# Expert weights into the [i1, i2, token] table: word writes by index in place of one-hot products

## The chip, the core and the metric

The kernel runs on one core of a Trainium2 chip. The metric is the device time of one execution in microseconds (us). The engines are named as in the profile: PE (TensorE, the matrix engine; PEld its weight loads), DVE (VectorE), ACT (ScalarE), POOL (GpSimd, which also issues all DMAs whose addresses come from an index), SP (SyncE, which issues most of the other DMAs). Each engine works through its own program in a fixed order; semaphores hold an instruction back until what it needs is there.

## The reference

One decoder block on 512 tokens of 1024 features, float32. Two mixers (a gated recurrence and dilated window attention) give a new x; behind a second norm (h2) comes the expert layer, which is where the change lies:

```python
q = (x @ w_q).reshape(B, S, 8, 2, 64)
s = einsum('bshpc,hpnc->bshpn', q, sub_keys)          # two halves, 128 keys each
s1, i1 = top_k(s[..., 0, :], 16); s2, i2 = top_k(s[..., 1, :], 16)
# top 16 of the 256 sums; expert number idx = i1 * 128 + i2; gate = softmax
hid = einsum('thkd,td->thk', u[idx], h2)              # 128 experts a token
a   = gelu(hid) * gate
out = einsum('thk,thkd->td', a, v[idx])               # added to x
```

So each token picks 128 pairs (8 heads of 16) out of 16384 experts, takes rows of u and v for them, and two heads of one token may pick the same expert.

## The kernel before, in words

The 512 tokens are four tiles (0 to 3) of 128. The mixers run in two halves (`Front(0)`, `Front(1)`, two tiles each); their weights arrive as 74 loads `w` on SP per half. The merge at the end of a half adds its two branches on POOL (L456, four adds), and what follows (output projection, h2, expert queries) waits for these adds.

The expert layer reaches the rows in two ways. By index: tile 0 gathers its rows of u, tile 3 its rows of u and v. Such a gather (`row`, L618) is one POOL instruction that fetches one row of 4 KB for each of 128 tokens; DVE multiplies and sums it (L626, L645). Streamed: tiles 1 and 2 need u whole, tiles 1, 2 and 0 need v whole. For a block b of 128 experts (128 blocks), `hidden(b)` loads `ub`, splits it into a high and a low half (`uh` on ACT, `ul` by a subtraction), and PE makes 24 products `ph` of 256 columns; ACT's gelu leaves them in `pre`, of which RING places exist. Then the loop over b loads `vb`, splits it into `vh` and `vl`, multiplies `pre[b]` by the gates `Gc` of that block (L825), splits the product into `ah` and `al`, and PE makes 18 products `acc` of 512 columns (L834). The acc products of a block need the gates of all three tiles.

That is what the table `g_d` is for: per token, the gate (tile 0: gate times gelu) of expert [i1, i2], and zero elsewhere. `scatter_steps` makes it from one-hot products: for four tokens at a time DVE compares a row of 0..127 with i1 and i2 (`e12`, L666) and multiplies by the weight's three bfloat16 thirds (`eg`, L670; ACT makes some thirds, L674), PE multiplies one-hot i1 by weighted one-hot i2 (12 products, L680), ACT copies the result to `Gx`, and SP writes `Gx` to DRAM. There are 32 such groups a tile, 96 in all: tile 1's beside the second half's mixers, those of tiles 0 and 2 beside the first `hidden` blocks. Products of one expert picked twice add up in PE.

`routing(T)` finds a tile's experts: DVE's top-16 instructions, `eq` (DVE), `sel` (POOL, L582 and L584) and `idf` (DVE). `Pump` objects (`rows`, `scat`) put steps of gathering and scattering between the other work. The order on each engine is then fixed when the kernel is built, by a scheduler that estimates durations.

Of the kernel before, what the change touches and what calls it, by code (L numbers as in the profile page):

```python
# [11 lines left out]
I32 = mybir.dt.int32  # L12
# [25 lines left out]
# Token tiles by how the expert layer reaches them: rows of u gathered, u streamed whole, v streamed whole.  # L38
# VD starts with UD; the tile that is not in it gathers its rows of v.
# [5 lines left out]
GT = 16  # L45
NGT = NV // GT
GB = 8
# the first weights' low halves are Pool's
LPOOL = 4
# steps of gathering and scattering before the end of the second half's mixers  # L50
ROWS_P, SCAT_PP = 99, 5
# [3 lines left out]
GS, EGB = 4, 2  # L55
ACT3 = {1: (0, 4, 8, 12), 0: (0, 4, 8, 12), 2: (0, 8)}
ROWS_F, ROWS_D, SCAT_F = 3, 2.0, 0.4
UK, WBUFS, ATB = 4, 4, 3

# columns of the packed per-partition parameters  # L60
C_G1, C_HGN, C_LB, C_QG, C_KG, C_END = 0, 8, 9, 17, 18, 19
# columns of the packed shape constants
M_ATT, M_HG, M_END = 0, 512, 640
# slots of the packed dense weights
# [4 lines left out]
def kernel(ctx: ExitStack, tc: tile.TileContext, x, wst, par, cst, cols, g2, keys, u, v, ut, vr, out):  # L69
# [9 lines left out]
    nc.scalar.activation(root, eps[:, 0:1], AF.Sqrt)  # L79
    h2g = {}  # L80
# [17 lines left out]
    def accumulate(out, ws, xs, cut, w_stays):  # L98
        """Sum over the blocks of w x, in three products where they come in two parts."""
# [24 lines left out]
    # lower bound: softmax over the two logit rows, row 0  # L124
# [5 lines left out]
    # values of the first group by token; of the other two with every fourth token's in a row  # L130
# [13 lines left out]
    class Front:  # L144
        """The mixers of one half of the tokens, and the queries of their expert layer."""

        def __init__(self, h, hi_pool, after_unit):
# [5 lines left out]
            for t in range(NT):  # L153
# [5 lines left out]
                for c in range(0, KC, 4):  # L159
# [20 lines left out]
        def slot(self, i, ks=slice(0, KC)):  # L180
            """Row blocks ks of a slot's weights, UK of them in a tile: the blocks' operands in order."""
# [14 lines left out]
        def proj(self, i, x, T):  # L196
            """A slot's 256 columns of the half's products with x, on the partitions (T) or along them."""
# [334 lines left out]
    def routing(T, rq):  # L532
# [66 lines left out]
        if T in VD:  # L599
# [6 lines left out]
            for j in range(2):  # L606
                nc.tensor.transpose(pt[:, 1 + j], i12[:, j], ident)
# [295 lines left out]
```

## Time and profile before

| | us |
|---|---|
| median of 3 timed runs | 1846.65 (1845.62 to 1847.0) |
| span of the profiled execution | 1845.0 |
| PE busy, share of the span | 1674.0, 91% |
| DVE busy | 1444.1, 78% |
| ACT busy | 795.6, 43% |
| POOL busy | 793.6, 43% |

The span runs from the first to the last instruction of the profiled execution; the profile gives no other time of its own for it. Busy time is an average over stages that differ: the first half's mixers fill PE from 0 to about 310 us, the second half's lie from there to about 700 us, the first `hidden` blocks and the scatter to 1066 us, the streamed products with v from 1066 us to the end.

### The profile page before, as it was taken

What the parts mean: (1) busy time and instruction counts of PE and PEld (TensorE: products, weight loads), DVE (VectorE), ACT (ScalarE), POOL (GpSimd) and SP (SyncE); (2) the same over time, 40 slices, a digit from 0 to 9 for tenths busy, and PEclk for the clock granted to TensorE, in tenths of its full rate; (3) what the DMA queues carried; (4) which work ended last, traced back from release to release, by engine and by line L of the source; (5) the groups of instructions that cost most, each with busy time, mean ns of one, the idle gap of its engine ahead of it and who ended that gap; (6) DMA issues with size and microseconds to landing.
All of it is one profiled execution on the core that took longest, in us unless ns stands there. A gap on an engine that the chain in (4) does not pass through costs nothing.

```text
span 1845.0 us, 28370 instructions
## 1 busy us (share of the span) xinstructions
PE 1674.0 (91%) x10573; PEld 1482.8 (80%) x10573; DVE 1444.1 (78%) x2681; ACT 795.6 (43%) x1348; POOL 793.6 (43%) x546
## 2 busy tenths in 40 slices
PE   6999889889789989888867899999999999999987
PEld 6998888667667878777867878888888888888766
DVE  5644547887887758999999977877877788888777
ACT  5655551211114556368756534343343434343232
POOL 3211312463664335556566543344323464444442
PEclk9999999988899989889978899999999999999999
DMA  6453553778787887534455799999988999999887
GB/s 196 153 158 119 175 194 118 270 235 276 244 279 264 297 298 261 183 111 145 152 183 202 238 372 334 339 328 326 367 298 299 345 339 341 340 340 317 288 309 278
DMA packets 169963, 475.61 MB, mean 258 GB/s; under 512 B 14304, under 2 KB 62688, under 8 KB 168800
## 3 DMA queue, kind: packets, MB, share of 16 engines
q1 hardware_dynamic: 112416, 270.56, 43.0%
q0 software_dynamic: 55296, 201.35, 30.9%
q10 hardware_dynamic: 2112, 1.88, 0.3%
q8 instruction: 83, 1.36, 0.3%
q14 instruction: 56, 0.46, 0.1%
HBM read 443.85 MB, written 28.84 MB: 256 GB/s over the span
## 4 chain that ended last, share of the span: by engine, by line
PE 47%; DVE 25%; DMA 11%; issue 9%; POOL 5%; ACT 1%; DVEq 0%; POOLq 0%; SPq 0%; ACTq 0%
PE acc L834 19%; PE pp L109 13%; PE ph L109 10%; DMA row<-in_u_dram,idx 6%; DVE row L626 4%; DVE e L666 4%; DVE eg L670 3%; POOL row L618 3%; DMA Gc<-g_d 3%; PE pg L680 2%; PE pr L680 1%; DVE cs L564 1%; DVE rest L515 1%; DVE ti L514 1%; DVE h2g L645 1%
## 5 line engine op out<-in xcount | busy, mean ns | idle before, releaser
L618 POOL DMA_INDIRECT row<-in_u_dram,idx x206 | 254.9, 1237 | 383.8 <-DVE row L626 274.3
L626 DVE SCALAR_TENSOR_TENSOR row<-row,h2g 128x1024 f32<-128x1024 f32 x206 | 272.4, 1328 | 62.2 <-DMA row<-in_u_dram,idx 61.3
L109 PE MATMUL ph<-hH,uh 128*128 128x256 f32 x1024 | 302.1, 295 | 7.1 <-ACT pre L792 6.0
L109 PE MATMUL ph<-hH,ul 128*128 128x256 f32 x1024 | 302.9, 296 | 5.0 <-POOL ul L95 5.0
L109 PE MATMUL ph<-hL,uh 128*128 128x256 f32 x1024 | 299.0, 292 | 0.0
L834 PE MATMUL acc<-vl,ah 128*128 128x512 f32 x768 | 241.8, 396 | 9.3 <-DVE vl L95 9.3
L834 PE MATMUL acc<-vh,al 128*128 128x512 f32 x768 | 240.0, 393 | 0.0
L94 ACT ACTIVATE uh<-ub 128x1024 fp32r<-128x1024 f32 x128 | 136.7, 1068 | 230.7 <-PE ph L109 214.1
L834 PE MATMUL acc<-vh,ah 128*128 128x512 f32 x768 | 222.5, 395 | 9.9 <-ACT vh L94 9.9
L109 PEld LDWEIGHTS ph<-hH,uh 128*128 128x128 f32 x1024 | 205.9, 201 | 12.8 <-ACT pre L792 7.8
L109 PEld LDWEIGHTS ph<-hH,ul 128*128 128x128 f32 x1024 | 205.5, 201 | 6.3 <-POOL ul L95 5.8
L109 PEld LDWEIGHTS ph<-hL,uh 128*128 128x128 f32 x1024 | 204.6, 200 | 3.8
L680 PEld LDWEIGHTS <-e 128*128 128x128 bf16 x1152 | 124.8, 119 | 73.4 <-DVE eg L670 65.4
L834 PEld LDWEIGHTS acc<-vl,ah 128*128 128x128 f32 x768 | 143.2, 190 | 40.0 <-DVE vl L95 11.8
L834 PEld LDWEIGHTS acc<-vh,ah 128*128 128x128 f32 x768 | 142.9, 190 | 38.2 <-ACT vh L94 10.5
L834 PEld LDWEIGHTS acc<-vh,al 128*128 128x128 f32 x768 | 145.5, 190 | 31.8
L94 ACT ACTIVATE ah<-Gc 128x384 fp32r<-128x384 f32 x128 | 66.9, 523 | 229.4 <-PE acc L834 226.7
L95 DVE TENSOR_TENSOR vl<-vb,vh 128x1024 fp32r<-128x1024 f32 x128 | 156.1, 1219 | 12.2 <-ACT vh L94 12.0
L618 POOL DMA_INDIRECT row<-in_v_dram,idx x76 | 111.6, 1469 | 120.0 <-DVE h2g L645 109.2
L680 PE MATMUL pg<-eg,e 128*128 128x128 bf16 x768 | 103.1, 297 | 51.8 <-DVE eg L670 51.3
L94 ACT ACTIVATE vh<-vb 128x1024 fp32r<-128x1024 f32 x128 | 135.6, 1059 | 28.6 <-DMA vb<-in_vr_dram 27.9
L674 ACT ACTIVATE eg<-e,pk 128x128 bf16<-128x128 bf16 x320 | 115.4, 565 | 70.9 <-DVE e L666 68.1
(279 smaller groups left out, 3582.4 us busy)
## 6 DMA issues: line engine op xcount, KB each, us to landing
w<-in_wst_dram SPq DMA_DIRECT2D x140, 512.0 KB
ub<-in_ut_dram SPq DMA_DIRECT2D x128, 512.0 KB
vb<-in_vr_dram SPq DMA_DIRECT2D x128, 512.0 KB
Gc<-g_d SPq DMA_DIRECT2D x15, 1536.0 KB
g_d<-Gx SPq DMA_DIRECT2D x16, 960.0 KB
g_d<-Gx SPq DMA_DIRECT2D x8, 1024.0 KB
row<-in_u_dram,idx POOLq DMA_INDIRECT x206
sc<-in_x_dram SPq DMA_DIRECT2D x4, 512.0 KB
```

Source lines behind the costliest of these rows:

```text
L94: nc.scalar.activation(hi, x, AF.Copy)
L95: (eng or nc.vector).tensor_tensor(out=lo, in0=x, in1=hi.bitcast(F32), op=ALU.subtract)
L109: nc.tensor.matmul(out, l, r, start=(i == 0), stop=(i == len(ops) - 1))
L514: nc.vector.max_index(out=ids[:, 0:8], in_max=vals[:, 0:8], in_values=src)
L515: nc.vector.match_replace(out=rest[:, :w], in_to_replace=vals[:, 0:8], in_values=src, imm_value=-BIG)
L618: nc.gpsimd.indirect_dma_start(out=r, out_offset=None, in_=src, in_offset=bass.IndirectOffsetOnAxis(ap=index, axis=0))
L626: nc.vector.scalar_tensor_tensor(r, r, 1.0, h2g[T], op0=ALU.mult, op1=ALU.mult, accum_out=hid[:, g, j:j + 1])
L666: nc.vector.tensor_tensor(out=e12, in0=iota[:, None].to_broadcast([P, 2, NKEY, GS]), in1=e[:, 0:2].to_broadcast([P, 2, NKEY, GS]), op=ALU. ...
L670: last_e2[0] = nc.vector.tensor_tensor(out=eg[:, :n], in0=e12[:, 1:2].to_broadcast([P, n, NKEY, GS]), in1=e[:, 2:2 + n].to_broadcast([P, n ...
L674: nc.scalar.activation(eg[:, 2, :, q], e12[:, 1, :, q], AF.Copy, scale=pk3[:, VD.index(T), i + k + q:i + k + q + 1])
L680: nc.tensor.matmul(pt[:, q], e12[:, 0, :, q0 + q], eg[:, j, :, q0 + q], start=(j == 0), stop=(j == 2))
L834: nc.tensor.matmul(acc[t][c], lt, r[:, c * 512:(c + 1) * 512], start=(b == 0 and i == 0), stop=(b == NKEY - 1 and i == 2))
```

## The change

Instead of one-hot products, each pair's weight is written to its place in the table by an indirect DMA of single words. The table is now three tensors [i1, i2, token] of 8 MB, one a tile. They are cleared first: twelve DMAs of 2 MB each from a tile of zeros, issued from ACT's queue behind every fourth weight load of the first half. For pair j of a tile, one DVE instruction compares all 128 expert numbers of a token with that of pair j and sums the weights of the equal ones (`same`, `wsum`), so that all writers of one place write the same sum; then one POOL instruction writes 128 words, one a token, to `place` = expert * 128 + token. That is 128 such pairs of instructions a tile, 384 in all. The 16 writes of a head wait for all 16 of the head before (`behind`), and the loads of `Gc` wait for a tile's last head. `ul` is DVE's in all blocks (before, POOL made it in the first 46), the blocks ahead of the products with v go from 46 to 60 and the places for `pre` from 58 to 72, and some gathers of tile 3 move ahead of the products with v.

```diff
-NPRE, RING = 46, 58
+ROWS_P, SCAT_PP = 99, 110
+NPRE, RING = 60, 72
+ROWS_F, ROWS_H, ROWS_D, SCAT_F = 3, 0.5, 1.9, 3
+RT3 = 16
...
         if T in VD:
-            pt = route_bank(T)
-            i12 = rt.tile([P, 2, P], F32, name="i12")
...
-                thirds(VD.index(T), pt[:, 3])
+            nc.vector.tensor_scalar(place[:, VD.index(T)], full, float(P), tok, op0=ALU.mult, op1=ALU.add)
...
-    def scatter_steps(T, bank):
...
+    def behind(d, others):
+        for o in others:
+            tc.add_manual_dep(d.ins, o.ins.name, mybir.DependencyInfo(mybir.DependencyClass.Sync, mybir.DependencyReason.DATA),
+                              reason="pairs of one expert")
+    def spread_steps(T):
+        i = VD.index(T)
+        w = gates[:, T] if T in UD else hid[:, UG.index(T)]
+        for j in range(P):
+            same = rt.tile([P, P], F32, name="same", bufs=2)
+            nc.vector.scalar_tensor_tensor(same, fulls[:, i], fulls[:, i, j:j + 1], w, op0=ALU.is_equal, op1=ALU.mult,
+                                           accum_out=wsum[:, i, j:j + 1])
+            d = nc.gpsimd.indirect_dma_start(out=g_d[i].rearrange("i j t -> (i j t)")[:, None], in_=wsum[:, i, j:j + 1],
+                                             out_offset=bass.IndirectOffsetOnAxis(ap=place[:, i, j:j + 1], axis=0),
+                                             in_offset=None)
...
+            if j % TOPK == 0:
+                before, spread[i] = spread[i], []
+            behind(d, before)
+            spread[i].append(d)
+            yield 1
...
+        def clearing(load):
+            if f_units[0] % 4 == 3 and clear:
+                g, k = clear.pop(0)
+                with tc.issue_after(load.ins):
+                    nc.scalar.dma_start(out=g[:, k:k + 32].rearrange("p (a b) t -> p a (b t)", b=8),
+                                        in_=zero[:, None].to_broadcast([P, 4, D]))
...
-    scat.add(scatter_steps(1, pr_bank))
+    scat.add(spread_steps(1))
...
+    scat.add(spread_steps(0))
...
-        ubs = halves(us.tile([P, KC, P], F32R, name="uh"), us.tile([P, KC, P], F32R, name="ul"), ub,
-                     nc.gpsimd if b < NPRE else nc.vector)
+        ubs = halves(us.tile([P, KC, P], F32R, name="uh"), us.tile([P, KC, P], F32R, name="ul"), ub)
...
+        scat.add(spread_steps(2))
+        scat(2 * P)
         for b in range(NPRE):
+            if b == RT3:
+                routing(3, rq3)
...
+            for t, g in enumerate(g_d):
+                behind(nc.sync.dma_start(out=Gc[:, t], in_=g[:, b:b + GB]), spread[t])
```

The scheduler lays the engines' programs out anew. On POOL, at the end of the second half's mixers, before (`row` is tile 0's gather, `pairA` the merge's add):

```order
L584 TENSOR_TENSOR sel<-sel 128x400
L618 DMA row<-in_u_dram,idx 128x1024 x18
L456 TENSOR_TENSOR pairA<-pairA,pairB 128x512 x2
L618 DMA row<-in_u_dram,idx 128x1024
L456 TENSOR_TENSOR pairA<-pairA,pairB 128x512
L618 DMA row<-in_u_dram,idx 128x1024
L456 TENSOR_TENSOR pairA<-pairA,pairB 128x512
L618 DMA row<-in_u_dram,idx 128x1024 x12
L95 TENSOR_TENSOR ul<-ub,uh 128x1024 x2
```

Now, at the same place (L599 is the gather, L646 the write of 128 words to tile 1's table, L457 the merge's add):

```order
L599 DMA row<-in_u_dram,idx 128x1024
L646 DMA g_d_113<-wsum,place 2097152x1 x2
L599 DMA row<-in_u_dram,idx 128x1024
L646 DMA g_d_113<-wsum,place 2097152x1 x5
L599 DMA row<-in_u_dram,idx 128x1024 x3
L646 DMA g_d_113<-wsum,place 2097152x1 x16
L599 DMA row<-in_u_dram,idx 128x1024 x3
L646 DMA g_d_113<-wsum,place 2097152x1 x16
L599 DMA row<-in_u_dram,idx 128x1024 x3
L457 TENSOR_TENSOR pairA<-pairA,pairB 128x512 x4
L646 DMA g_d_113<-wsum,place 2097152x1 x11
L599 DMA row<-in_u_dram,idx 128x1024
```

The merge's adds come behind 83 gathers and 48 word writes (39 of these writes stand above), where before 94 gathers and no write stood ahead of the first of them; 80 word writes of tile 1 are still to come. Further down on POOL, beside the first `hidden` blocks, before (`ul` is the low half of a block of u, `Gc` the copy of the table's first blocks):

```order
L687 COPY Gc<-Gx 128x128
L95 TENSOR_TENSOR ul<-ub,uh 128x1024 x2
L582 TENSOR_TENSOR sel<-eq,ci 128x800
L584 TENSOR_TENSOR sel<-sel 128x400
L95 TENSOR_TENSOR ul<-ub,uh 128x1024
L582 TENSOR_TENSOR sel<-eq,ci 128x800
L687 COPY Gc<-Gx 128x128
L95 TENSOR_TENSOR ul<-ub,uh 128x1024
L584 TENSOR_TENSOR sel<-sel 128x400
L582 TENSOR_TENSOR sel<-eq,ci 128x800
L95 TENSOR_TENSOR ul<-ub,uh 128x1024
```

Now (`g_d_115` is tile 0's table, `g_d_114` tile 2's; `row` and `rq` are tile 3's gathers, L574 and L576 its routing):

```order
L646 DMA g_d_115<-wsum,place 2097152x1 x16
L574 TENSOR_TENSOR sel<-eq,ci 128x800
L599 DMA row<-in_u_dram,idx 128x1024 x3
L599 DMA rq<-in_u_dram,idx 128x1024 x2
L576 TENSOR_TENSOR sel<-sel 128x400
L646 DMA g_d_115<-wsum,place 2097152x1 x16
L574 TENSOR_TENSOR sel<-eq,ci 128x800
L599 DMA row<-in_u_dram,idx 128x1024 x3
L599 DMA rq<-in_u_dram,idx 128x1024 x2
L646 DMA g_d_114<-wsum,place 2097152x1
L646 DMA g_d_115<-wsum,place 2097152x1 x16
L646 DMA g_d_114<-wsum,place 2097152x1 x13
```

The `ul` and `Gc` rows are gone from POOL; 384 word writes, the last 57 gathers of tile 0 and the first 45 of tile 3 stand between the first and the last word write of the program. Each Pool DMA also waits on one of eight semaphores, that of the DMA eight before it. On SP, around the first loads of `Gc`:

```order
L770 DMA ub<-in_ut_dram 128x1024 x5
L187 DMA w<-in_wst_dram 128x1024 x4
L770 DMA ub<-in_ut_dram 128x1024 x12
L799 DMA Gc<-g_d_113 128x1024
L770 DMA ub<-in_ut_dram 128x1024 x20
L784 DMA h2g<-h_d 128x1024
L770 DMA ub<-in_ut_dram 128x1024 x41
L799 DMA Gc<-g_d_115 128x1024
L799 DMA Gc<-g_d_114 128x1024
L804 DMA vb<-in_vr_dram 128x1024 x3
L799 DMA Gc<-g_d_113 128x1024
```

The gates of tiles 0 and 2 stand behind 78 loads of `ub`. On PE the same shows as 1776 `ph` products (74 blocks) ahead of the first `acc` product, against 1248 (52 blocks) before.

## Rows read from the trace of the kernel before

**Rows 1.** Busy time by engine in stretches; then PEclk, DMA share, GB/s.

```profile
100.00:200.00 100.00, 100.00 (x1007) 93.71 (x1007) 44.87 (x85) 56.28 (x101) 14.86 (x7) 1.00 0.46 143
760.00:1050.00 290.00, 232.31 (x1737) 220.12 (x1737) 280.10 (x624) 187.66 (x348) 172.13 (x103) 0.87 0.48 161
1060.00:1440.00 380.00, 375.12 (x2135) 328.90 (x2134) 298.62 (x446) 147.97 (x208) 144.32 (x108) 0.99 0.94 333
```

**Rows 2.** PE's waits, 740 to 1066 us: total, times, longest.

```profile
PE pg L680 <- DVE eg L670: 51.3, 25, 9.8
```

**Rows 3.** PE groups from 0 to 1066 us: busy, mean ns, idle before.

```profile
L109 PE MATMUL ph<-hL,uh 128*128 128x256 f32 x416 | 127.2, 306 | 0.0
```

**Rows 4.** PE groups from 1066 us to the end.

```profile
L109 PE MATMUL ph<-hL,uh 128*128 128x256 f32 x608 | 171.9, 283 | 0.0
```

**Rows 5.** Line 834, the products with v: ns min/median/max, first and last start.

```profile
L834 PE MATMUL acc<-vh,ah x768: 387/389/797, 1066.2 to 1832.4; 128*128 128x512 f32 x192
...
L834 PE MATMUL acc<-vh,al x768: 387/389/628, 1074.9 to 1835.1; 128*128 128x512 f32 x192
```

**Rows 6.** Line 666, the first one-hot operand: same columns.

```profile
L666 DVE TENSOR_TENSOR e<-iota,pk x96: 660/686/3107, 567.5 to 1044.1; 128x1024 bf16<-128x1024 bf16 x96
```

**Rows 7.** PE in order of time, 1100 to 1115 us: start, duration.

```profile
1106.02 1.55 PE L834 MATMUL acc<-vh,ah 128*128 128x512 f32 x6
1107.41 0.28 PE L109 MATMUL ph<-hH,ul 128*128 128x256 f32 x1
1107.53 0.28 PE L109 MATMUL ph<-hH,uh 128*128 128x256 f32 x1
```

**Rows 8.** POOL groups over the span.

```profile
L618 POOL DMA_INDIRECT row<-in_u_dram,idx x206 | 254.9, 1237 | 383.8 <-DVE row L626 274.3 <-DVE ti L517 16.8 <-DVE tv L516 16.8
...
L582 POOL TENSOR_TENSOR sel<-eq,ci 128x800 f32<-128x800 bf16 x32 | 54.5, 1704 | 56.1 <-DVE eq L580 55.9
L584 POOL TENSOR_TENSOR sel<-sel 128x400 f32<-128x400 f32 x32 | 40.8, 1276 | 0.7
```

**Rows 9.** POOL in order of time, 655 to 725 us: start, duration, idle before.

```profile
674.66 1.80 POOL L618 DMA_INDIRECT row<-in_u_dram,idx  x1 [4.81 <-DVE row L626]
676.77 0.94 POOL L618 DMA_INDIRECT row<-in_u_dram,idx  x1 [0.30 <-issue]
678.01 0.94 POOL L618 DMA_INDIRECT row<-in_u_dram,idx  x1 [0.30 <-PE pp L109]
```

**Rows 10.** POOL in order of time, 1180 to 1240 us.

```profile
1186.58 1.68 POOL L618 DMA_INDIRECT row<-in_u_dram,idx  x1 [2.71 <-DVE row L626]
1188.56 1.67 POOL L618 DMA_INDIRECT row<-in_u_dram,idx  x1 [0.30 <-issue]
```

**Rows 11.** DVE in order of time, 655 to 760 us.

```profile
682.04 2.69 DVE L626 SCALAR_TENSOR_TENSOR row<-row,h2g 128x1024 f32<-128x1024 f32 x1 [5.15 <-DMA row<-in_u_dram,idx]
```

**Rows 12.** DVE, tile row, 655 to 725 us: ns min/median/max, first and last start.

```profile
L626 DVE SCALAR_TENSOR_TENSOR row<-row,h2g x19: 1210/1225/3326, 663.7 to 720.2; 128x1024 f32<-128x1024 f32 x19
```

**Rows 13.** DMA queues: packets, MB, share of 16 engines' span.

```profile
q1 hardware_dynamic: 112416, 270.56, 43.0%
q0 software_dynamic: 55296, 201.35, 30.9%
```

**Rows 14.** DVE groups, 740 to 1062 us.

```profile
L666 DVE TENSOR_TENSOR e<-iota,pk 128x1024 bf16<-128x1024 bf16 x62 | 75.7, 1227 | 6.8 <-PE pg L680 6.6
L670 DVE TENSOR_TENSOR eg<-e,pk 128x1024 bf16<-128x1024 bf16 x64 | 74.7, 1171 | 0.0
...
L95 DVE TENSOR_TENSOR ul<-ub,uh 128x1024 fp32r<-128x1024 f32 x7 | 9.4, 1346 | 0.0
...
L626 DVE DVE_READ_ACCUMULATOR rq<-rq,h2g 128x1 f32 x17 | 1.3, 76 | 0.0
```

**Rows 15.** Line 605, a 128x128 scalar_tensor_tensor on DVE.

```profile
L605 DVE SCALAR_TENSOR_TENSOR i<-i,full x3: 272/285/293, 399.2 to 883.5; 128x128 f32<-128x128 f32 x3
```

**Rows 16.** Line 456, the merge's adds on POOL.

```profile
L456 POOL TENSOR_TENSOR pairA<-pairA,pairB x8: 1283/1956/2245, 218.3 to 610.8; 128x512 f32<-128x512 f32 x8
```

More of the change, by code (lines that the diff above doesn't have):

```diff
@@ L79 @@
     nc.scalar.activation(root, eps[:, 0:1], AF.Sqrt)
+    tok = const.tile([P, 1], F32, name="tok")
+    nc.scalar.dma_start(out=tok, in_=par[:, C_TOK:C_TOK + 1])
     h2g = {}
@@ L521, in route_bank @@
         return pt.rearrange("p (n k) -> p n k", k=NKEY)
-    def thirds(i, x):
-        w, dst = pk3[:, i], pk[:, i, 2:]
-        nc.vector.tensor_copy(dst[:, 0], x)
-        nc.vector.tensor_tensor(out=w, in0=x, in1=dst[:, 0], op=ALU.subtract)
-        nc.vector.tensor_copy(dst[:, 1], w)
-        nc.vector.tensor_tensor(out=w, in0=w, in1=dst[:, 1], op=ALU.subtract)
-        nc.vector.tensor_copy(dst[:, 2], w)
     def routing(T, rq):
         gate = gates[:, T]
-        full = rt.tile([P, P], F32, name="full")
+        full = fulls[:, VD.index(T)] if T in VD else rt.tile([P, P], F32, name="full")
         sv = rt.tile([P, PH, TOPK], F32, name="sv")
@@ new lines @@
+    spread = {i: [] for i in range(len(VD))}
+    def behind(d, others):
[12 more added lines that the diff above has]
+                                             in_offset=None)
+            tc.declare_no_dep(d.ins, group=f"spread{i}{j // TOPK}", reason="heads are ordered below")
+            tc.add_to_no_dep_group(f"spread{i}{j // TOPK}", d.ins)
+            if j % TOPK == 0:
+                before, spread[i] = spread[i], []
+            behind(d, before)
+            spread[i].append(d)
@@ L711 @@
     rows, scat = Pump(), Pump()
+    dram = ctx.enter_context(tc.tile_pool(name="dram", bufs=1, space=bass.MemoryType.DRAM))
+    h2_d = dram.tile([P, D], F32, name="h2_d")
+    g_d = [dram.tile([P, NKEY, P], F32, name=f"g_d{i}") for i in range(len(VD))]
     rq_pool = ctx.enter_context(tc.tile_pool(name="rq", bufs=2, side="left"))
@@ L715 @@
     with tc.tile_pool(name="whi", bufs=5, side="left") as whi:
-        f = Front(0, whi, lambda load: None)
+        zero = whi.tile([P, D], F32, name="zero", bufs=1)
+        nc.gpsimd.memset(zero, 0.0)
+        clear = [(g, k) for g in g_d for k in range(0, NKEY, 32)]
+        def clearing(load):
[4 more added lines that the diff above has]
+                                        in_=zero[:, None].to_broadcast([P, 4, D]))
+            f_units[0] += 1
+        f_units = [0]
+        f = Front(0, whi, clearing)
         with tc.issue_after(f.last_norm.ins):
@@ L778 @@
     pre = []
-    Gcs = [dp.tile([P, NGT, GB, GT], F32, name="Gc")]
-    nc.sync.dma_start(out=Gcs[0][:, :P // GT], in_=g_d[:, :P // GT, :GB])
     def hidden(b, pool):
@@ L792, in hidden @@
         nc.scalar.activation(dst, pt, AF.Gelu)
-    with tc.tile_pool(name="php", bufs=2, space=PSUM, side="right") as php, \
-            tc.tile_pool(name="pg", bufs=3, space=PSUM, side="right") as pg:
-        pg_bank = lambda: pg.tile([P, 512], F32, name="pg")
+    with tc.tile_pool(name="php", bufs=4, space=PSUM, side="right") as php:
         routing(2, rq2)
-        scat.add(scatter_steps(0, pg_bank))
-        scat.add(scatter_steps(2, pg_bank))
-        scat(P)
+        scat.add(spread_steps(2))
+        scat(2 * P)
         for b in range(NPRE):
-            hidden(b, php)
-        routing(3, rq3)
-    h2g[3] = const.tile([P, D], F32, name="h2g")
-    nc.sync.dma_start(out=h2g[3], in_=h2_d)
-    rows.add(u_steps(3))
-    with tc.issue_after(last_e2[0].ins):
-        rows(4)
+            if b == RT3:
+                routing(3, rq3)
+                h2g[3] = const.tile([P, D], F32, name="h2g")
+                nc.sync.dma_start(out=h2g[3], in_=h2_d)
+                rows.add(u_steps(3))
+            hidden(b, php)
+            rows(ROWS_H)
     rows.add(v_steps(3))
```

76 lines of the change are left out of this document (11 added, 65 removed).

## The prediction

> **What bounds the kernel now.** I read the stretches first [rows 1]. In the streamed part (1060 to 1440 us) PE is busy 375 of 380 us at almost full clock: there PE's own work is the length. In the stretch ahead of it, 760 to 1050 us, PE is busy 232 of 290 us at a clock share of 0.87, and DVE 280 of 290 us: there DVE is the bound. PE's waits say the same: 51.3 us, all for `eg`, the weighted one-hot product on DVE [rows 2]. So the profile splits at the first product with v, at 1066.2 us [rows 5]. What comes before it is a race to have the table of gates complete; what comes after is PE's work.
>
> The second part can be priced by its pitch. Six `acc` products take 1.39 us from the first to what follows (0.232 us each), and a `ph` product follows the last after 0.12 us [rows 7]. A block of v is 18 `acc` products (4.17 us), a block of u 24 `ph` products (2.88 us). By 1066 us PE has done 416 * 3 of the latter, which is 52 blocks [rows 3]; 76 are left [rows 4]. That makes 128 * 4.17 + 76 * 2.88 = 753 us; from 1066.2 us to the last product at 1835.1 us [rows 5], which ends some 0.4 us later, it took 769 us. The loss is 16 us, and another 9.5 us lie between that end and the span's. I work against the span, 1845.0 us; the median of the runs lies 1.65 us above it.
>
> **The change, part by part.** The end is therefore (first product with v) + (v's products and the u blocks then left) + 16 + 9.5. The new order has 74 u blocks ahead of the first `acc` product, all that the 72 places of `pre` let PE make, so 54 are left: 128 * 4.17 + 54 * 2.88 = 689 us, which with 25.5 makes 715 us. The question is when the table is complete.
>
> *What is removed.* 96 `e12` and 96 `eg` instructions on DVE, 1.23 and 1.17 us each beside POOL's work [rows 14], 1152 one-hot products on PE, ACT's thirds and copies, POOL's 46 `ul` and 16 copies. PE's 51 us of waiting go with them. None of this is a gain unless the table is ready sooner.
>
> *What is added on POOL.* Each word write is an indirect DMA over 128 indices, as a gather is. No word write is in this trace; the nearest row is the gather: 206 of them at a mean of 1.237 us [rows 8]. What one costs POOL is more than that, since 0.30 us pass between two of them: 676.77 to 678.01 us, 1.24 us a piece, when undisturbed [rows 9]; 1.98 us when DVE reads two operands at the same time [rows 10]. Does it become cheaper because a word is moved and not a row of 4 KB? The software queue counted 55296 packets for 384 gathers, 144 for each [rows 13]: 128 for the rows and 16 more. A gather is already one descriptor a row whatever its length, so 128 words are as many. The lower bound is therefore 1.24 us, the upper the mean, 1.237 + 0.30 = 1.54 us (1.98 us if DVE disturbed every one). I take the middle, 1.39 us: DVE is full beside the first half of these writes and has run out of work beside the second.
>
> *When they can start.* Tile 1's writes need tile 1's routing, as the first one-hot operand did at 567.5 us [rows 6]; nothing that the change takes away lies ahead of that, so I start at 565 us. From there to the last word write POOL's new order holds 384 writes, 57 gathers of tile 0 and 45 of tile 3, which is 486 indirect DMAs: 486 * 1.39 = 676 us. Then 16 pairs of `sel` at 1.70 + 1.28 us [rows 8], 48 us, and the merge's four adds at 1.96 us [rows 16], 8 us. The last 24 gathers of tile 0 run with no word writes between them, and there landing sets the pace: 19 followed at (720.2 - 663.7) / 18 = 3.1 us [rows 12], so 24 * (3.1 - 1.39) = 41 us more. Tile 0's weights need the gelu behind these gathers, so its 128 writes and, behind them in the queue, tile 2's come last.
>
> *The waits between heads.* A gather issued at 674.66 us was used at 682.04 us, 7.4 us later [rows 9, 11]; a word write moves a thousandth of that and lands sooner, between 0 and 7.4 us. Nearly every head is followed on POOL by gathers, `sel` or the other tile's head, which cover it; I count five bare joints at 3 us, 15 us (0 to 24 * 7.4 = 178 us at the ends). While POOL waits, everything behind it in its queue waits too, the gathers included, and DVE waits for those. The Trainium skill, page "DMA: Bandwidth & Descriptors", section "Anatomy of one DMA — SWDGE (gpsimd) path", puts about 2 us fixed cost on such a DMA, mostly the receipt of the write, so that 24 joints would cost at most 48 us; that is 33 us above my 15.
>
> *Sum for the table.* 565 + 676 + 48 + 8 + 41 + 15 = 1353 us for the last write. Its landing, the load of `Gc`, the multiplication and the split add about 10 us, no row for the whole of it (0 to 20). First product with v: 1363 us.
>
> *Hidden parts.* DVE's 384 `same` cost 0.285 us [rows 15] and 0.076 us for reading the sum [rows 14], 0.36 us, 139 us in all; 107 us of it (297 instructions), 70 more `ul` at 1.35 us (94 us) and 36 more gathered rows at 1.3 us (47 us) come behind the second half's h2, where 76 `e12` and `eg` pairs at 2.40 us (182 us) go away. DVE is then 66 us longer there than before, which would put the table at 1066 + 66 = 1132 us: hidden behind POOL, by 220 us. PE's 74 blocks (213 us) are hidden in the same way; PE idles for some 300 us. The merge's adds come behind 48 word writes and end some 45 us later than at 611 us [rows 16]; this delays h2 and the u blocks, but nothing that POOL waits for. The loads of `ub` behind tile 1's `Gc` on SP wait for tile 1's last word; that is covered too.
>
> *The clearing.* 25.2 MB. The hardware queue took 43.0% of the span, 793 us of all 16 engines, for 270.56 MB [rows 13]; the clearing is then 74 us of them, in a half whose DMA share is about 0.46 while PE is full [rows 1]. It fits; I take 5 us (0 to 25).
>
> *Total.* 1363 + 715 + 5 = 2083 us of span; with 1.65 us for the median, 2085 us, 13% slower.
>
> **The rivals.**
>
> *Cheap words (not slower).* If POOL needed far less than a gather's time for a write of words, DVE would be the bound as worked out above: first product at 1132 us or, without POOL's `ul` beside DVE (the `e12` of that stretch took 1.23 us, its median over the run 0.69 us [rows 6, 14]), some 40 us sooner. End: 1132 + 715 + 5 = 1852 down to 1812 us. The point from which it decides: for 1846 us the last write has to come at 1116 us, 551 us from the start, less 112 us for `sel`, adds and waits and 102 gathers at 1.39 us (142 us), leaves 297 us for 384 writes, 0.77 us each. The shortest pitch in the trace is 1.24 us. The skill speaks for this rival: in the section named above it calls descriptor generation small, with many descriptors before the cost shows. This trace disagrees for gathers of 128 rows, 1.237 us on POOL at the mean; no run here shows words.
>
> *Slow landing (much slower).* Eight Pool DMAs can be on their way at once. With the gather's 7.4 us that allows one every 0.92 us, less than POOL's own pitch, so it does not bind. If a write of 128 words took 16 us to land it would be 2.0 us a piece: 384 * 0.61 = 234 us more, 2319 us. Against it: few bytes. In favour: the words go to 128 scattered places in DRAM, and no row shows such a write. The same page ("Specifications") has transfers under 512 bytes read, modified and written back, which speaks for this side.
>
> *POOL undisturbed (milder).* At 1.24 us for every DMA: 486 * 0.15 = 73 us less, 2012 us; without the bare joints, the landing, the slow gathers and the clearing, 1940 us.
>
> **How the numbers follow.** The forecast with its milder form has 0.76, cheap words 0.10, slow landing 0.12; 0.02 goes to a price between 0.77 and 1.24 us, slower too. The predicted time is the forecast's. The upper end of the range takes the mean pitch (486 * 0.15 = 73 us) and a third of slow landing (78 us): 2240 us. The lower end is the milder form without its extras, 1940 us; what is left out is cheap words and the worst of slow landing. Slower by over 0.2% (3.7 us, about what a measurement of this kernel can tell): 0.90; faster 0.07, same 0.03, both from cheap words.
>
> **What would show it.** Right: a group of 384 word writes on POOL at about 1.0 to 1.3 us each with 0.3 us ahead of them; POOL without long pauses from 565 to about 1350 us; PE's first `acc` product at about 1360 us behind a wait of some 300 us that ends with a Pool DMA; behind it 715 us as priced. Wrong: writes at under 0.8 us, with DVE full until the first `acc` product (cheap words); long idle time ahead of the writes, ended by DMAs (slow landing); or the writes of tile 1 starting well before 565 us, which would pull the whole queue forward.

## The result and the profile after

The changed kernel takes 2133.41 us (median of 4 runs, 2130.72 to 2159.99), the kernel before beside it 1846.83 us: a ratio of 1.158 with a 95% interval of 1.151 to 1.165, slower. The forecast was 2085 us in a range of 1940 to 2240. The profiled execution has a span of 2130.1 us, against which the readings below are made.

The page of the changed kernel, its first two parts (busy time of each engine, then the span in 40 slices of 53 us):

```profile
span 2130.1 us, 26658 instructions
PE 1571.0 (74%) x9412; PEld 1375.1 (65%) x9412; DVE 1380.9 (65%) x3279; ACT 598.2 (28%) x932; POOL 1068.2 (50%) x869
PE   0899989888856768688772000019999999999998
DVE  1454457988845337799694152228888888888994
POOL 1221132445675765648787757774444343335540
PEclk9999999889867878899886555559999999999999
DMA  9744454777734645674361112339999999998994
```

Most of the loss can be seen in the row of PE: four slices with nothing and one on either side with little, where the kernel before was streaming. In these slices no engine is busier than POOL, and DVE has little to do in most of them. Two other things strike the eye: PE's first slice is empty too, beside a DMA share of 9 tenths, and the granted clock falls while PE stands still. The same by stretches (columns as in [rows 1]):

```profile
1100.00:1300.00 200.00, 24.71 (x179) 22.99 (x177) 85.62 (x351) 13.45 (x18) 145.85 (x137) 0.59 0.25 78
1300.00:1400.00 100.00, 0.00 (x0) 0.00 (x0) 23.29 (x39) 0.00 (x0) 79.33 (x75) 0.50 0.27 86
1500.00:1800.00 300.00, 300.00 (x1698) 263.91 (x1698) 247.35 (x336) 118.95 (x169) 122.77 (x92) 1.00 0.93 339
```

PE's longest waits (columns as in [rows 2]: total, times, longest):

```profile
PE ph L110 <- ACT pre L774: 312.7, 12, 295.8
PE pp L110 <- ACT hH L95: 40.0, 1, 40.0
```

The products with v, as [rows 5]:

```profile
L810 PE MATMUL acc<-vh,ah x768: 387/389/497, 1435.8 to 2121.2; 128*128 128x512 f32 x192
L810 PE MATMUL acc<-vh,al x768: 387/389/632, 1437.6 to 2123.9; 128*128 128x512 f32 x192
```

The wait of 295.8 us for `pre` means that all 72 places are full. None comes free until the gates have arrived and DVE has multiplied the first block by them; one more block of u then runs from 1431.3 us, and the first product with v follows at 1435.8 us (1066.2 before). So the span again splits in two: 1435.8 us until the table is there, and 694.3 us behind it.

What fills the first part is POOL. Its groups from the first word write to the end of the last one, 584.6 to 1424.2 us (busy time, mean ns, then the idle time ahead and what ended it):

```profile
L646 POOL DMA_INDIRECT g_d<-wsum,place x384 | 418.6, 1090 | 125.2 <-issue 103.9 <-DMA g_d<-wsum,place 10.2 <-DVE same L644 5.9
L599 POOL DMA_INDIRECT row<-in_u_dram,idx x84 | 98.5, 1172 | 94.9 <-DVE row L607 30.4 <-DVE ti L518 19.0 <-issue 13.5
L574 POOL TENSOR_TENSOR sel<-eq,ci 128x800 f32<-128x800 bf16 x16 | 27.2, 1700 | 23.7 <-DVE eq L572 23.2 <-issue 0.3
L599 POOL DMA_INDIRECT rq<-in_u_dram,idx x18 | 20.0, 1110 | 5.5 <-issue 4.9 <-DVE full L583 0.3 <-DVE same L644 0.3
L576 POOL TENSOR_TENSOR sel<-sel 128x400 f32<-128x400 f32 x16 | 19.7, 1233 | 0.6
L457 POOL TENSOR_TENSOR pairA<-pairA,pairB 128x512 f32<-128x512 f32 x4 | 5.9, 1508 | 0.0
```

The six rows add up to 840 us, the whole stretch. Words are 544 us of it, 1.416 us each with the idle time ahead of them. POOL's own waits in this stretch, added up by what ended them, are 114 us for DVE and 11 us for a DMA; DVE for its part waits 81.5 us there for gathered rows to land and 65.0 us for POOL's `sel`. So POOL is the engine with the least room, but it doesn't run without pauses. Undisturbed, late in the chain, words follow one another every 1.27 us:

```profile
1329.20 0.96 POOL L646 DMA_INDIRECT g_d<-wsum,place  x1 [0.30 <-issue]
1330.47 0.97 POOL L646 DMA_INDIRECT g_d<-wsum,place  x1 [0.30 <-issue]
```

The empty first slice is the clearing. ACT's queue in order of time (start, duration, what), 4 to 52 us:

```profile
8.56 5.07 ACTq L696 DMA_DIRECT2D g_d<-zero  x1
13.68 0.29 ACT L142 ACTIVATE st<-st,eps 128x1 f32<-128x1 f32 x1 [4.07 <-issue]
13.70 16.16 ACTq L696 DMA_DIRECT2D g_d<-zero  x3
29.91 1.06 ACT L95 ACTIVATE wh<-w 128x1024 fp32r<-128x1024 f32 x1 [15.94 <-issue]
```

All twelve clears are issued between 4.5 and 52.1 us; from the fourth on, one issue holds ACT for about 5 us, and ACT's halves of the first weights and of x come out between them. The anchor of a clear is a load in SP's queue, the clear itself is ACT's: all twelve are among the first 27 instructions that the profile has of ACT and its queue, so nothing spreads them.

### The profile page after: what moved, and what is told of

It reads as the page before. It is cut to its first block, busy times and chain, and to the rows that moved or that the text cites. A ratio compares the mean times of both kernels' runs of the same rounds, so it can differ in the third digit from the quotient of the medians.

```text
span 2130.1 us, 26658 instructions
## 1 busy us (share of the span) xinstructions
PE 1571.0 (74%) x9412; PEld 1375.1 (65%) x9412; DVE 1380.9 (65%) x3279; ACT 598.2 (28%) x932; POOL 1068.2 (50%) x869
## 3 DMA queue, kind: packets, MB, share of 16 engines
q0 software_dynamic: 67584, 201.57, 27.4%
## 4 chain that ended last, share of the span: by engine, by line
PE 49%; DVE 16%; POOL 8%; issue 7%; DMA 7%; another core or an unknown queue 5%; ACT 1%; DVEq 0%; SPq 0%; POOLq 0%; ACTq 0%
PE acc L810 24%; PE ph L110 13%; PE pp L110 10%; POOL g_d L646 5%; DMA row<-in_u_dram,idx 5%; DVE row L607 4%; DVE same L644 3%; DVE ul L96 2%; POOL row L599 1%; DMA w<-in_wst_dram 1%; DVE idf L577 1%; DMA vb<-in_vr_dram 1%; POOL rq L599 1%; DVE rest L516 1%
## 5 line engine op out<-in xcount | busy, mean ns | idle before, releaser
L110 PE MATMUL ph<-hH,uh 128*128 128x256 f32 x1024 | 307.5, 300 | 333.6 <-ACT pre L774 312.7
L646 POOL DMA_INDIRECT g_d<-wsum,place x384 | 418.6, 1090 | 125.2 <-issue 103.9
L110 PEld LDWEIGHTS ph<-hH,uh 128*128 128x128 f32 x1024 | 210.6, 206 | 344.2 <-ACT pre L774 315.5
L599 POOL DMA_INDIRECT row<-in_u_dram,idx x206 | 248.7, 1207 | 276.2 <-DVE row L607 139.6
L96 DVE TENSOR_TENSOR ul<-ub,uh 128x1024 fp32r<-128x1024 f32 x128 | 165.0, 1289 | 113.3 <-ACT uh L95 99.4
L110 PEld LDWEIGHTS ph<-hH,ul 128*128 128x128 f32 x1024 | 210.2, 206 | 40.1 <-DVE ul L96 32.2
L110 PEld LDWEIGHTS ph<-hL,uh 128*128 128x128 f32 x1024 | 210.5, 206 | 6.4 <-issue 3.7
L810 PE MATMUL acc<-vh,ah 128*128 128x512 f32 x768 | 210.7, 391 | 5.1 <-ACT vh L95 5.1
L96 POOL TENSOR_TENSOR wl<-w,wh 128x1024 fp32r<-128x1024 f32 (+1 forms) x22 | 55.2, 2508 | 247.8 <-ACT wh L95 194.0
L599 POOL DMA_INDIRECT row<-in_v_dram,idx x76 | 103.1, 1356 | 113.7 <-DVE h2g L622 102.6
```

Of the source, the lines that this page charges most:

```text
L96: (eng or nc.vector).tensor_tensor(out=lo, in0=x, in1=hi.bitcast(F32), op=ALU.subtract)
L110: nc.tensor.matmul(out, l, r, start=(i == 0), stop=(i == len(ops) - 1))
L599: nc.gpsimd.indirect_dma_start(out=r, out_offset=None, in_=src, in_offset=bass.IndirectOffsetOnAxis(ap=index, axis=0))
L646: d = nc.gpsimd.indirect_dma_start(out=g_d[i].rearrange("i j t -> (i j t)")[:, None], in_=wsum[:, i, j:j + 1], out_offset=bass.IndirectOff ...
L810: nc.tensor.matmul(acc[t][c], lt, r[:, c * 512:(c + 1) * 512], start=(b == 0 and i == 0), stop=(b == NKEY - 1 and i == 2))
```

## The experiments

Each kernel is the changed one with the edit shown, except the three whose names begin with `words_`, which start from the kernel before. A single run of this kernel can lie 30 us off (2130.72 to 2159.99 above), so of kernels with one run only the trace's own times and larger differences are read.

**clear_paced.** The clears go out of SP's queue.

```
-                    nc.scalar.dma_start(out=g[:, k:k + 32]...
+                    nc.sync.dma_start(out=g[:, k:k + 32]...
```

> The twelve clears go out of SP's queue, one behind every fourth load of weights, instead of out of ACT's. Theory (the clears fill the DMA engines ahead of the first weights and block ACT, and everything behind them, POOL's chain of words too, starts 48 us later): the first pp product at about 20 us, the first half's h2 near 256 us, the first word write at about 540 us, the first acc product at about 1390 us, span about 2085 us (2078 to 2100). Rival one (POOL's chain starts late for another reason, the clearing is hidden): the first word write stays at 585 us and the span at 2130. Rival two (25 MB take DMA time from the weights wherever they are queued): h2 between 280 and 330 us, span 2110 to 2150.

2065.3 us (4 runs, 2059.9 to 2072.53), ratio to before 1.115 [1.111, 1.119]. Stretches of the changed kernel:

```profile
0.00:40.00 40.00, 3.90 (x16) 3.13 (x16) 5.55 (x19) 7.00 (x11) 6.26 (x9) 1.00 0.97 382
40.00:80.00 40.00, 16.68 (x109) 15.58 (x110) 6.05 (x10) 11.50 (x14) 7.07 (x3) 0.99 0.96 386
```

The same of this one:

```profile
0.00:40.00 40.00, 26.61 (x185) 25.95 (x185) 20.44 (x33) 22.10 (x29) 17.18 (x13) 1.00 0.92 333
40.00:80.00 40.00, 38.54 (x313) 36.30 (x311) 24.66 (x32) 22.36 (x32) 5.47 (x3) 1.00 0.84 312
80.00:260.00 180.00, 170.39 (x1536) 160.70 (x1534) 85.31 (x135) 93.03 (x162) 37.66 (x17) 0.97 0.65 227
```

PE works from the start, at a DMA share that is still high: the first half's h2 comes at 261.0 us (304.0 in the changed kernel, 256.0 before), so the same 25 MB beside the same weights cost 5 us once they are in the order of the loads. The first word comes at 541.7 us (584.7) and the first product with v at 1378.2 us (1435.8). The span is 59 us shorter, 14 us more than expected; the two rivals fall. The edit does two things at once, it spreads the clears and takes them out of ACT's queue, and no run separates these. In the changed kernel PE's first long wait, the 40.0 us shown above, ended with ACT's `hH`, which stood behind the clears.

**half_heads.** The pairs of every second head are left out, sums and writes.

```
         for j in range(P):
+            if j // TOPK % 2:
+                continue
```

> The pairs of every second head are left out (192 word writes and their sums on DVE fewer; the table then holds half of the pairs). Theory (POOL's queue of indirect DMAs sets when the table is complete): 192 * 1.42 = 272 us less, the first acc product near 1165 us, span near 1860 us, a little more if DVE becomes the bound first. Rival (DVE is the bound, POOL only follows): DVE loses 192 * 0.44 = 84 us, span near 2045 us. Rival (waits between heads): 12 of the 24 joints go, at the measured 10 us in all that is 5 us.

Span 1852.4 us (one run, 1854.2 us). The 192 writes lie between 587.7 and 1130.4 us, 543 us instead of 839: 296 us for 192 writes. The span is 278 us shorter, where 272 was expected of POOL's queue and 84 of DVE's sums alone.

**half_tokens and tokens_8.** Each write takes the first 64, or 8, of its 128 indices; the other tokens' pairs are left out.

```
-            d = nc.gpsimd.indirect_dma_start(..., in_=wsum[:, i, j:j + 1], ... ap=place[:, i, j:j + 1] ...
+            d = nc.gpsimd.indirect_dma_start(..., in_=wsum[:64, i, j:j + 1], ... ap=place[:64, i, j:j + 1] ...
```

> Each word write takes the indices of 64 tokens instead of 128 (384 writes as before; the other tokens' pairs are left out). If POOL's price of an indirect DMA is fixed for each DMA: 1.09 us and 0.33 us ahead of it stay, span 2130 us. If POOL's price goes by the number of indices: near 0.55 us, the pitch falls by about 0.5 us or more, 384 * 0.5 = 190 us less, span near 1940 us. In between, a line through both points gives a fixed part and a price of an index.

> Each word write takes the indices of 8 tokens instead of 128 (the other tokens' pairs are left out; 384 writes as before). The shortest write took 0.967 us with 128 indices and 0.892 us with 64. If the price is a fixed part and a small part for each index, the line gives 0.892 - 56 * 0.00117 = 0.826 us with 8, and the span stays above 2080 us. If it falls in proportion below 64 indices: near 0.11 us, pitch 0.4 us, and the span near that of few_words plus the clearing's 59 us, 1830 us.

The word writes of the changed kernel (ns min/median/max, first and last start):

```profile
L646 POOL DMA_INDIRECT g_d<-wsum,place x384: 965/969/2008, 584.7 to 1423.0; - x192
```

Of half_tokens:

```profile
L646 POOL DMA_INDIRECT g_d<-wsum,place x384: 892/897/1941, 581.2 to 1427.6; - x192
```

Of tokens_8:

```profile
L646 POOL DMA_INDIRECT g_d<-wsum,place x384: 844/853/1912, 583.8 to 1418.0; - x192
```

Sixteen times fewer indices make a write 0.12 us shorter, 0.97 to 0.85 us at the median; the line through the first two points would have given 0.826 at its shortest, it was 0.844. Most of the price belongs to the DMA, not to the words in it.

The spans stay (2138.7 and 2130.2 us), though the price did fall somewhat. POOL's two largest groups of tokens_8, from the first word to the last, show where that went:

```profile
L646 POOL DMA_INDIRECT g_d<-wsum,place x384 | 370.7, 965 | 145.9 <-issue 112.0 <-DVE same L644 25.6 <-DVE ti L515 6.1
L599 POOL DMA_INDIRECT row<-in_u_dram,idx x84 | 95.5, 1137 | 108.8 <-DVE row L607 28.4 <-DVE same L644 28.4 <-DVE ti L518 15.4
```

POOL is busy with words for 48 us less (370.7 against the changed kernel's 418.6 us), yet the last word starts only 5 us sooner: POOL's waits for DVE grow from 114 to 162 us in all. Faster writes alone gain nothing here. What is worth saving is the number of writes, and the diff has no lever on that: one write is one column of pairs.

**ul_on_pool.** The lower halves of u's first 60 blocks go back to POOL.

```
-    ubs = halves(..., us.tile([P, KC, P], F32R, name="ul"), ub)
+    ubs = halves(..., us.tile([P, KC, P], F32R, name="ul"), ub,
+                 nc.gpsimd if b < NPRE else None)
```

> The 60 lower halves of the streamed weights ahead of the products with v go back from DVE to POOL, 40 of them ahead of the last word write in POOL's order. Theory (POOL is the bound up to the first acc product): 40 * 2.54 us (their price on POOL before the change) = 102 us more, span near 2230 us (2200 to 2260). Rival (DVE is the bound): 40 * 1.34 = 54 us less, span near 2076 us.

Span 2289.6 us, 160 us more, where 102 were expected. All 60 stand ahead of PE's first product with v, 142.4 us of POOL with 16.2 us of waits, since the blocks of u that they belong to come first. PE shows it:

```profile
PE ph L110 <- POOL ul L96: 393.1, 31, 65.8
```

The direction is the theory's, the place of the cost was not. The 41 halves ahead of the last word take 105 us of POOL with their waits, but the chain of words gets only 23 us longer (587.5 to 1449.1 us), since POOL's waits for DVE fall from 114 to 75 us and the words and gathers themselves go faster. The rest comes behind the last word: the end hangs on the last of POOL's pieces that the first product needs.

**few_words.** As clear_paced, but of each head only the first write is issued (24 of 384); all sums stay.

```
+            if j % TOPK:
+                yield 1
+                continue
             d = nc.gpsimd.indirect_dma_start(out=g_d[i]...
```

> With the clears paced as in the run clear_paced, and only the first of each head's 16 word writes issued (24 instead of 384; the other pairs are left out of the table). All sums on DVE stay. This asks what would bind if words cost POOL next to nothing. Prediction's rival (DVE is then the bound): the first acc product between 1090 and 1132 us, span 1812 to 1852. If landing of tile 0's gathers is the next bound (3.1 us each with three to five buffers): 128 gathers from 327 us on end near 327 + 128 * 3.1 = 724 us, before tile 2's routing on DVE, so that DVE decides again, but earlier: first acc product between 950 and 1050 us, span 1730 to 1800. If POOL's words were not the cause after all: span stays near 2070.

Span 1767.2 us (one run, 1769.1 us): 78 us shorter than the kernel before, and 304 us shorter than clear_paced. The stretches ahead of its first product with v, at 1089.8 us:

```profile
780.00:900.00 120.00, 111.09 (x874) 108.09 (x872) 119.02 (x535) 51.72 (x78) 23.68 (x18) 0.97 0.50 161
900.00:1020.00 120.00, 62.78 (x407) 58.91 (x406) 115.16 (x333) 25.24 (x37) 82.02 (x62) 0.78 0.85 298
1020.00:1089.00 69.00, 26.00 (x168) 24.34 (x168) 63.64 (x146) 11.11 (x18) 50.14 (x37) 0.71 0.74 254
```

DVE (the third engine in these rows) is now full, 298 of 309 us. So with next to no writes DVE is the bound, and the change, with its clears paced, would have paid.

**rows3_behind.** The gathers of tile 3 stand behind the last word.

```
-ROWS_F, ROWS_H, ROWS_D, SCAT_F = 3, 0.5, 1.9, 3
+ROWS_F, ROWS_H, ROWS_D, SCAT_F = 3, 0, 2.0, 3
...
-        rows(ROWS_D)
+        with tc.issue_after(spread[1][-1].ins):
+            rows(ROWS_D)
```

> The 45 gathers of tile 3 that stand ahead of the last word write in POOL's order stand behind it. Theory (every indirect DMA ahead of the last word counts): 45 * 1.47 = 66 us less for the table, first acc product at 1370 us. Behind it 256 gathers are left instead of 211; in the changed kernel these took 640 us, 3.03 us each, so 256 take 776 us and the last one ends at about 2146 us, behind the last acc product (1370 + 688 = 2058 us): span about 2150 us, ended by DVE's gathered rows and not by PE. Rival (the gathers ran in pauses between heads and cost the table nothing): first acc product stays at 1436 us, span 2200 us or more.

The first product with v comes at 1379.0 us, 57 us sooner for 45 gathers, but the span is 2123.2 us. DVE's last gathered row starts at 2107.4 us, behind the last product with v at 2068.3:

```profile
L622 DVE SCALAR_TENSOR_TENSOR h2g<-row,hid,h2g x76: 1270/1280/1324, 1795.7 to 2107.4; 128x1024 f32<-128x1024 f32 x76
```

As expected, to within 27 us: what the table gains is given back by gathers that no longer fit beside PE's second part.

**sel_paced and sel_late.** As clear_paced, with POOL's `sel` pairs on DVE: all 32 (`nc.vector` in both lines), or those of tiles 2 and 3 (shown).

```
-                nc.gpsimd.tensor_tensor(out=sel, in0=eq, in1=ci...
+                (nc.vector if T > 1 else nc.gpsimd).tensor_tensor(out=sel, in0=eq, in1=ci...
-                nc.gpsimd.tensor_add(sel[:, :hc]...
+                (nc.vector if T > 1 else nc.gpsimd).tensor_add(sel[:, :hc]...
```

> The clears paced as in the run clear_paced, and the 32 pairs of sel and its folding add on DVE instead of POOL. Theory (POOL is the bound): against clear_paced 16 pairs * (1.69 + 1.26) = 47 us and their 15 us of waiting for DVE go from POOL, first acc product at about 1315 us, span about 2010 us (1990 to 2030). Rival (DVE is the bound): 16 pairs on DVE at 1.3 us or more add 20 us or more to 2071 us.

> As sel_paced, but only the sel pairs of tiles 2 and 3 go to DVE, the 16 that lie between the first and the last word on POOL; tiles 0 and 1 keep theirs on POOL. In sel_paced the 63 us that left POOL gave nothing: the first word came 33 us later (tile 1's routing was longer on DVE), and in the chain from first to last word 50 us came back as waits for DVE. If the first loss was tile 1's routing: the first word stays at 542 us here. The chain then decides: in POOL's order 14 more gathers of tile 3 stand ahead of the last word than in clear_paced (14 * 1.47 = 21 us), so with the 50 us of waits again the span is near 2071 - 63 + 50 + 21 = 2079 us; if the waits for DVE were tile 1's doing too: near 2071 - 63 + 21 = 2029 us.

sel_paced: 2080.87 us (4 runs, 2069.35 to 2090.44), ratio 1.124 [1.119, 1.129], against 1.115 [1.111, 1.119] of clear_paced: no gain, and my expectation of 2010 us failed. sel_late: 2070.58 us, ratio 1.120 [1.116, 1.125], not to be told from clear_paced. POOL's groups from the first word to the last, of clear_paced:

```profile
L646 POOL DMA_INDIRECT g_d<-wsum,place x384 | 407.6, 1061 | 139.2 <-issue 106.7 <-DVE same L644 23.3 <-DMA g_d<-wsum,place 6.5
L599 POOL DMA_INDIRECT row<-in_u_dram,idx x84 | 99.2, 1181 | 83.2 <-DVE row L607 29.2 <-DVE sv L517 16.2 <-issue 13.6
L574 POOL TENSOR_TENSOR sel<-eq,ci 128x800 f32<-128x800 bf16 x16 | 27.1, 1691 | 15.4 <-DVE eq L572 15.3
```

Of sel_paced:

```profile
L646 POOL DMA_INDIRECT g_d<-wsum,place x384 | 414.2, 1079 | 148.8 <-issue 111.2 <-DVE same L644 30.1 <-DMA g_d<-wsum,place 4.5
L599 POOL DMA_INDIRECT row<-in_u_dram,idx x76 | 81.0, 1066 | 129.5 <-DVE row L607 36.6 <-DVE same L644 28.8 <-DVE rest L516 22.4
```

In sel_paced the chain from the first word to the last is only 13 us shorter (574.9 to 1384.6 us against 541.7 to 1364.4), though 63 us of `sel` with its waits have gone: gathers wait 46 us longer (129.5 against 83.2 us, nearly all of it for DVE), words 10 us. And the chain starts 33 us later. sel_late keeps its start (first word at 544.8 us), as expected of tile 1's routing, and comes within 6 us of the sum with the returned waits (span 2073.3 us, 2079 expected). So POOL's queue is the bound only together with what DVE hands it: POOL has no slack to give and DVE, in this stretch, not much either.

**words_one_tile, words_late, words_late_ul.** The kernel before with tile 1's 128 words written by indirect DMAs into a table of its own (8.4 MB, cleared out of SP's queue); tiles 0 and 2 keep their one-hot products. Buffers and the loads of `Gc` are moved to suit. In the second kernel the words stand behind tile 0's last gather, in the third every third `ul` goes to DVE as well.

```
-    scat.add(scatter_steps(1, pr_bank))
+    words.add(spread_steps())
...
     with tc.issue_after(f.last_h2.ins):
         rows(2 * P)
-        scat(P)
+    with tc.issue_after(last_row[0].ins):
+        words(P)
...
-                     nc.gpsimd if b < NPRE else nc.vector)
+                     nc.gpsimd if b < NPRE and b % 3 else nc.vector)
```

> The kernel of before with word writes for tile 1 alone (128 of them, a table of its own of 8.4 MB cleared out of SP's queue, the words landing in the layout of the one-hot table); tiles 0 and 2 keep their one-hot products. In the kernel of before POOL waited most of 560 to 750 us, so 128 * 1.42 = 182 us of words fit there if the theory of POOL's queue holds. DVE loses 32 pairs of e12 and eg (77 us, 29 us of them behind the second half's h2) and gains 128 sums (56 us); PE loses 384 products. Theory: first acc product at 1040 to 1066 us with a few more u blocks done ahead of it, span 1800 to 1845 us. Rival (gathers and words get into each other's way on POOL, tile 0's weights come later than DVE frees): 1850 to 1900 us.

> As words_one_tile, but tile 1's 128 words are issued behind tile 0's last gather in POOL's order, not among the gathers. In words_one_tile tile 0's weights came at 922 us instead of 772 and the first acc product at 1189 us. Theory (a word costs what stands behind it in POOL's queue, 1.42 us each): tile 0's weights come back to about 772 us, the last word at about 1010 us, tile 2's sel, now among the words, 100 us later than before; first acc product 1050 to 1110 us, span 1810 to 1880 us. Rival (what delayed words_one_tile was DVE's sums or PE, not POOL's order): tile 0's weights stay above 850 us and the span near 1960 us.

> As words_late, with every third ul of the first 46 streamed blocks on DVE, which takes 16 * 2.54 = 41 us from POOL and gives DVE 16 * 1.34 = 21 us. If POOL is the bound between 770 and 1066 us in words_late: span 20 to 40 us below it. If DVE is the bound there, as in the kernel before: 10 to 25 us above it.

1966.87 us, ratio 1.065 [1.061, 1.069]; 1956.72 us, 1.058 [1.056, 1.061]; 1928.87 us, 1.044 [1.041, 1.048]. All slower than before. The first is beyond both figures that I gave; the second ends where its rival put it, near 1960 us, but not with the late weights of tile 0 that the rival had as its sign. Tile 0's gelu, which its weights need, starts at 772.5 us in the kernel before. In words_one_tile (first start; the last is tile 3's):

```profile
L667 ACT ACTIVATE hid<-hid x2: 309/310/312, 922.0 to 1534.4; 128x128 f32<-128x128 f32 x2
```

In words_late:

```profile
L667 ACT ACTIVATE hid<-hid x2: 302/306/309, 744.6 to 1522.0; 128x128 f32<-128x128 f32 x2
```

Words among the gathers hold tile 0 up by 150 us; behind them they don't, and yet words_late is hardly faster. Its words end at 986 us (1010 expected), but tile 2's `sel` pairs and the `ul` now wait in POOL's queue among them. The stretch 740 to 960 us of words_late:

```profile
740.00:860.00 120.00, 63.12 (x413) 55.72 (x414) 75.48 (x259) 59.22 (x124) 85.98 (x77) 0.61 0.23 76
860.00:960.00 100.00, 44.85 (x294) 40.85 (x293) 47.71 (x114) 36.66 (x70) 74.07 (x67) 0.65 0.20 62
```

The kernel before had PE busy 98.5 and 77.3 us there, DVE 115.7 and 99.0, POOL 74.1 and 60.9: POOL has gained, and DVE and PE have lost. Two waits of words_late from 640 to 1190 us, 5.0 us and under 2 us in the kernel before, say what they wait for:

```profile
PE ph L112 <- POOL ul L98: 68.6, 11, 19.8
DVE idf L588 <- POOL sel L587: 39.9, 2, 21.1
```

Taking 41 us of `ul` from POOL then gives 28 us (expected 20 to 40 if POOL is the bound there, a loss if DVE is). No version that writes all its pairs beat the kernel before.

## Why the prediction was right, and where its sum was off

The mechanism held in the main: the table is complete when POOL has issued its queue of indirect DMAs, PE stands with 72 full places until then, and the rest is PE's pitch. What the sum left out is that POOL also waits for DVE, 114 of the 840 us. The terms, in the order of the sum:

- **Start, 565 us.** Measured 584.7, and 541.7 in clear_paced. Two errors met and partly cancelled, by luck: the clearing costs 43 us at this point, and without it tile 1's first word is ready 23 us sooner than I had put it, 26 us sooner than its one-hot operand was [rows 6]. That transposes and thirds no longer stand ahead of it is an argument for this, not shown.
- **Words, 1.39 us each.** Measured 1.416 with all idle time ahead of the words, from a bare pitch of 1.27: right, though its reason was not. I took a write to be as many descriptors as a gather, from the count of packets. The software queue counts 67584 packets now and 55296 before [rows 13]; 12288 more for 384 writes are 32 for each, not 144. half_heads (61440, for 192 writes) and both runs with fewer indices (67584) give the same 32. POOL's time does not follow the packets, and the indices hardly: a gather of 144 packets went out every 1.24 us undisturbed [rows 9], a write of 32 every 1.27 us.
- **Gathers, 102 * 1.39 + 41 = 183 us.** Measured 219 us (98.5 + 94.9 + 20.0 + 5.5): 100 us of waiting, of which 30.4 are for rows that DVE still holds and 19.0 end with `ti`, an instruction of the top-16 search that stands in DVE's queue. I had priced landing alone.
- **`sel`, 48 us.** Measured 71: 23.2 us of waiting for `eq` on DVE were not in it. Adds 6 (8).
- **Waits between heads, 15 us.** Measured 10.2 in 6 waits, the longest 4.7; they are already within the words' 1.416. The Trainium skill, page "DMA: Bandwidth & Descriptors", section "Anatomy of one DMA — SWDGE (gpsimd) path", puts most of about 2 us on the receipt of a write. What POOL still had to wait for here was 1.7 us at the mean of the six, which agrees in size; the longest, 4.7 us, is above it, and no run shows the receipt by itself.
- **From the last word to the first product, 10 us.** Measured 12 (1424.0 to 1435.8).
- **Second part, 715 us.** Measured 694. By 1435.8 us PE had done 592 * 3 / 24 = 74 blocks of u, as predicted, and against 128 * 4.17 + 54 * 2.88 = 689 us, 688 us passed up to the last product's start, 1435.8 to 2123.9 us. The 16 us of loss in the kernel before did not come again, and the tail was 5.8 us, not 9.5.
- **Clearing, 5 us.** This is the step that failed: "it fits" was argued from a mean DMA share of 0.46 and 74 us of all engines, as if the transfers were spread over the half. They were not; they came in one piece beside the first weights and held up ACT. 59 us by clear_paced; paced, they cost the 5 us that I had taken, at the first half's h2.

Together: 2083 + 20 (start) + 51 (10 for words, 36 for gathers, 23 for `sel`, less the 15 between heads, which the words now hold, and 2 for the adds, rounded) + 2 - 21 (second part) - 5 (clearing, which now sits in the start) = 2130 us.

Of the rivals, slow landing is out (10.2 us), and POOL undisturbed too (1.416 us a word). Cheap words did not happen, but few_words shows that its working was sound: the first product at 1089.8 us, where 1092 to 1132 had been worked out ("some 40 us sooner" than 1132), DVE full ahead of it. Its span, 1767 us, lies below the 1812 to 1852 us given there, since 80 blocks of u were done by then, not 74, and since the second part's loss is gone (677 us, not 715). The break-even of 0.77 us a write agrees with half_heads, where half the writes at the full price, 289.5 us in all (297 at the break-even), end 7 us behind the kernel before. That is in part luck: the bunched clearing is still in it, the first word comes 23 us later than the 565 us of the working, and the second part is 29 us shorter than its 715 us (686.3). The Trainium skill, page "DMA: Bandwidth & Descriptors", section "Anatomy of one DMA — SWDGE (gpsimd) path", has many descriptors emitted before their cost shows; for the number of indices the runs agree, 0.12 us for 120 of them. The whole is another matter: a write of 8 words still takes POOL 0.844 us, and 0.30 us pass to the next.

Of what I named as hidden, PE's 74 blocks were: PE had done all but the last of them by 1135.5 us. The last of the merge's adds starts at 687.4 us instead of 610.8 [rows 16]; in clear_paced it starts at 642.0 us, so 45 us of this go with the clearing. DVE's work was not hidden: POOL waits 114 us for it, tokens_8 gives back in such waits what POOL saves, and sel_paced loses by more work on DVE. That DVE was below full in the mean, 86 of 200 us from 1100 to 1300 us, doesn't show that POOL never waits for it.

Open is why the chain of clear_paced is 16 us shorter than that of the changed kernel beyond its earlier start (823 against 839 us): the waits differ by such amounts between kernels whose order differs little, and no run separates them.

## What to carry to other kernels

Price an indirect DMA by the piece on the engine that issues it, 1.27 us undisturbed here, and count pieces: 384 of them on one in-order queue outweighed 192 wide vector instructions and 1152 products that ran on engines side by side. A background transfer is hidden only if something paces it, so check that its anchor is in the same queue; twelve clears that fit by bandwidth cost 59 us when they all left at once, out of a queue whose engine the first products needed. And where two engines hand work to each other in order, relieving the busier one, by moving its pieces or by making them shorter, can come back as waits for the other: look at what ends its waits first.

## What the runs showed of the hardware that I had not expected

- POOL's time for an indirect write depended little on the number of indices: 0.844, 0.892 and 0.965 us at the shortest for 8, 64 and 128, and each write counts 32 packets in the queue, whichever it is.
- A DMA issue can hold up the engine that issues it: the twelve clears took ACT's queue 4.96 us each at the median and 10.1 at most, while the DMA engines were 97% busy, and ACT's own work waited behind them. Out of SP's queue, spread over 5.2 to 168.1 us, the same twelve took 0.43 us each.
- While PE stood still its granted clock was 0.50 (1300 to 1400 us), the lower of its two levels (1.2 GHz of 1.2 and 2.4). The block of u that PE made right behind the pause still ran at that level, 0.21 us a product up to 1434.7 us and 0.12 us behind it; it took 4.4 us instead of 2.88, so the return cost 1.5 us, all of it ahead of the first product with v:

```profile
1431.30:1434.60 3.30, 3.26 (x15) 3.26 (x16) 3.30 (x8) 1.46 (x2) 0.98 (x1) 0.50 1.03 416
1434.70:1435.70 1.00, 1.00 (x10) 1.00 (x10) 1.00 (x2) 0.90 (x1) 0.00 (x0) 1.00 1.07 410
```
